# A chunked state recurrence: its small products of two tiles and two heads put on different quarters of the matrix array, and its state kept without zero blocks

## The chip, the cores and the metric

The kernel runs on one core of a Trainium2 chip. A core has a matrix engine (TensorE, PE in the profile, with PEld for its weight loads), VectorE (DVE), ScalarE (ACT), GpSimd (POOL) and SyncE (SP, which issues the transfers here). The metric is the device time of one execution in microseconds (us), the median of several runs.

## The reference

Two layers of width 2048 over 256 tokens. The first layer's mixer is the recurrence with which the change deals: per head of 64, a state S of 64 x 64 that is decayed, corrected by a rank-one term and fed with v k at each token.

```python
def step(S, inp):
    r_t, w_t, k_t, v_t, a_t, b_t = inp
    sa = jnp.einsum('bhij,bhj->bhi', S, a_t)
    S = S * w_t[:, :, None, :] + sa[..., None] * b_t[:, :, None, :] + v_t[..., None] * k_t[:, :, None, :]
    y = jnp.einsum('bhij,bhj->bhi', S, r_t)
    return S, y
```

Around it stand projections of x (r, k, v and three low-rank ones), a group norm per head, a gate, an output projection, a layer norm and a gated MLP; the second layer has differential attention in the place of the recurrence. All is float32 in and out.

## The kernel before

Activations lie with features on the 128 partitions, 16 feature tiles of 128 x 256 tokens. The large products ("dense" below) split each float32 operand into two parts, hi and lo: weights arrive in `raw` by a transfer, ScalarE casts them to `hi` (L210), VectorE or, for every fourth piece in the recurrence, GpSimd subtracts to get `lo` (L213), and TensorE multiplies (L221 to L223, or L225 and L226, into the tile `psd`).

The recurrence works on 8 groups of 2 feature tiles (index `jj`), that is 4 heads (2 per tile, index `h`, in partition rows 0 to 63 and 64 to 127), in 4 chunks of 64 tokens (index `c`). A group passes through four stages: `products` (dense, r and k), `front` (gates, decays; L1127 multiplies keys by queries in each chunk into `pss`, and L1129 masks that into `M`), `lanes` (the inverse of each chunk's 64 x 64 triangle, by small products L1217 to L1244, kept in `M`) and `chain` with `outputs`. In `pipeline` four groups are in work at once, one in each stage (the conditions for the first and last steps are left out here):

```python
todo.append((_then(self.chain(i), self.outputs(i)), PACE["chain"], PACE["chain0"]))
todo.append((self.lanes(i + 1), PACE["lanes"], PACE["lanes0"]))
todo.append((self.front(i + 2), PACE["front"], PACE["front0"]))
todo.append((self.products(i + 3), PACE["products"], PACE["products0"]))
```

`_together` interleaves these generators at their `yield`s, and the tile framework's scheduler then fixes each engine's order when the program is built; every engine runs its list in that order. In the last two steps `early` (first parts of the output projection, dense too) takes the place of the stages that have run out.

One chunk of `chain` is: rp = AR S + M v (L1295 and L1298, for each tile one and two products), a copy of rp to `R` (ScalarE), up = M R (L1303), a copy of up into `UV` (VectorE), then the new state from `KBT` and `UV` (L1310, and L1316 or L1320 on VectorE) and the outputs `yps` (L1324 from S, L1326 from UV). S is kept as [128, 2 tiles, 2 heads, 64] with a zero block where row half and head differ, so that one product of 128 rows serves both heads of a tile. rp and up of a chunk lie in 64 partitions, the same half for both tiles. In PSUM the recurrence has six banks: `pss` for front (2), lanes (1) and chain (1), `yps` (1) and `rp` (1); the dense products have two of their own.

A float32 product of this stage stands in the trace as two instructions (four calls at L1303 are "x8").

## Time and profile before

| | us |
|---|---|
| median of 3 runs | 2617.95 |
| the runs | 2612.49, 2617.95, 2630.53 |
| the profiled execution: its own time | 2630.53 |
| its span, first to last instruction | 2630.5 |
| TensorE busy in it | 2524.3 (96%) |
| VectorE busy | 2067.1 (79%) |
| ScalarE busy | 1642.4 (62%) |

The profiled execution is the slowest of the three runs. The recurrence's first product of a chain starts at 168.8 us and its last at 661.8 us; the rest of the time is dense products before and after it. A busy TensorE is not one at its peak: many of its busy nanoseconds in the recurrence belong to products that use a quarter of the array. Rows of the timeline give an instruction's start, and the distance of starts tells what it costs in a queue that never empties.

### The profile page before, as it was taken

Reading aid. Unit: us, or ns where it says so; the run is one execution under the profiler, and the core shown is the slowest. Engines: PE = TensorE matmul, PEld = TensorE weight load, DVE = VectorE, ACT = ScalarE, POOL = GpSimd, SP = SyncE. Lnnn points to the kernel's source line nnn. Section 1 sums busy time; section 2 is a strip of 40 time slices with the busy share of each in tenths; the row PEclk is TensorE's granted clock in tenths of the full one; section 3 lists DMA queues with packets and bytes.
Section 4 is the critical chain, followed back from the end, with each engine's and each line's share of the span. In section 5 each row is a group of like instructions: output and inputs, shape, how many; then the busy total and the mean of one; then the engine's idle time right before and its main releaser. Section 6 shows DMA issues by size and latency. Waiting matters only on the chain.

```text
span 2630.5 us, 54371 instructions
## 1 busy us (share of the span) xinstructions
PE 2524.3 (96%) x17374; PEld 2220.6 (84%) x17374; DVE 2067.1 (79%) x5108; ACT 1642.4 (62%) x4287; POOL 379.8 (14%) x457
## 2 busy tenths in 40 slices
PE   7999999999899999998899999999999999999997
PEld 6888888877788888887788999998888888888886
DVE  8977888885898777775677887778897777777776
ACT  5766455553566666664566676666676666666664
POOL 4343333331220000000111200002300000000112
PEclk9999999998999999999899999999999999999998
DMA  5544333343446555555666455555465555556664
GB/s 187 173 126 122 88 96 101 101 108 91 134 151 199 190 190 190 188 190 145 191 189 191 147 177 176 169 173 184 143 201 189 188 188 188 188 187 185 190 189 129
DMA packets 285160, 429.60 MB, mean 163 GB/s; under 512 B 69064, under 2 KB 91592, under 8 KB 284872
## 3 DMA queue, kind: packets, MB, share of 16 engines
q1 hardware_dynamic: 284872, 426.12, 53.4%
q8 instruction: 136, 2.23, 0.3%
q14 instruction: 152, 1.25, 0.2%
HBM read 419.45 MB, written 6.56 MB: 162 GB/s over the span
## 4 chain that ended last, share of the span: by engine, by line
PE 86%; DVE 7%; DMA 3%; issue 2%; ACT 1%; POOL 1%; SPq 0%; DVEq 0%; ACTq 0%; POOLq 0%
PE psd L225 41%; PE psd L226 21%; PE psd L221 3%; PE psd L223 3%; PE psd L222 3%; DVE lo L213 2%; PE pss L1127 1%; DMA raw<-in_ff_down 1%; PE psd L293 1%; PE psd L291 1%; PE psd L292 1%; DVE mx L767 1%; PE psd L891 1%; PE psd L892 1%; PE psd L890 1%
## 5 line engine op out<-in xcount | busy, mean ns | idle before, releaser
L210 ACT CAST hi<-raw 128x256 fp32r<-128x256 f32 (+1 forms) x3128 | 1229.3, 404 | 730.2 <-PE psd L225 470.8
L213 DVE TENSOR_TENSOR lo<-raw,hi 128x256 fp32r<-128x256 f32 (+1 forms) x2984 | 1291.9, 444 | 423.6 <-ACT hi L210 388.0
L225 PE MATMUL psd<-S,hi 128*128 128x512 f32 x3004 | 1058.6, 396 | 0.1
L226 PE MATMUL psd<-S,lo 128*128 128x256 f32 x3004 | 842.8, 281 | 3.4 <-DVE lo L213 3.2
L225 PEld LDWEIGHTS psd<-S,hi 128*128 128x128 f32 x3004 | 567.0, 189 | 132.6 <-ACT hi L210 1.1
L226 PEld LDWEIGHTS psd<-S,lo 128*128 128x128 f32 x3004 | 566.6, 189 | 5.0 <-DVE lo L213 3.7
L225 PE MATMUL psd<-hs,hi 128*128 128x512 f32 x1290 | 452.9, 395 | 22.7 <-ACT hi L210 22.7
L226 PE MATMUL psd<-hs,lo 128*128 128x256 f32 x1290 | 362.4, 281 | 0.7 <-DVE lo L213 0.6
L225 PEld LDWEIGHTS psd<-hs,hi 128*128 128x128 f32 x1290 | 242.7, 188 | 79.1 <-ACT hi L210 23.4
L226 PEld LDWEIGHTS psd<-hs,lo 128*128 128x128 f32 x1290 | 244.1, 189 | 1.6 <-DVE lo L213 1.5
L363 POOL COPY ln_acc<-X 128x256 f32<-128x256 f32 x4 | 2.1, 526 | 1257.4 <-DVE X L397 1257.4
L213 POOL TENSOR_TENSOR lo<-raw,hi 128x256 fp32r<-128x256 f32 x144 | 121.8, 852 | 330.2 <-ACT hi L210 253.4
L223 PE MATMUL psd<-S,lo 128*128 128x256 f32 x480 | 139.4, 290 | 15.6 <-DVE lo L213 10.0
L221 PE MATMUL psd<-S,hi 128*128 128x256 f32 x480 | 141.2, 294 | 1.5 <-ACT hi L210 1.5
L222 PE MATMUL psd<-S,hi 128*128 128x256 f32 x480 | 136.0, 283 | 0.0
L225 PE MATMUL psd<-S1r,hi 128*128 128x512 f32 x276 | 108.9, 425 | 1.3 <-DVE S1r L192 0.7
L223 PEld LDWEIGHTS psd<-S,lo 128*128 128x128 f32 x480 | 90.9, 189 | 22.4 <-DVE lo L213 14.7
L370 POOL TENSOR_TENSOR ln_acc<-ln_acc,X 128x256 f32<-128x256 f32 x49 | 40.2, 820 | 402.1 <-DVE X L409 388.6
L221 PEld LDWEIGHTS psd<-S,hi 128*128 128x128 f32 x480 | 91.1, 190 | 5.6 <-ACT hi L210 1.9
L222 PEld LDWEIGHTS psd<-S,hi 128*128 128x128 f32 x480 | 91.1, 190 | 1.7 <-issue 1.5
L221 PE MATMUL psd<-S1r,hi 128*128 128x256 f32 x284 | 87.7, 309 | 0.0
L891 PE MATMUL psd<-S,lo 128*128 128x258 f32 x256 | 77.2, 301 | 9.8 <-DVE lo L213 9.8
(295 smaller groups left out, 3921.5 us busy)
## 6 DMA issues: line engine op xcount, KB each, us to landing
raw<-in_ff_up SPq DMA_DIRECT2D x676, 256.0 KB, 3.4
raw<-in_ff_down SPq DMA_DIRECT2D x320, 256.0 KB, 2.9
raw<-in_rkv SPq DMA_DIRECT2D x192, 256.0 KB, 3.4
raw<-in_da_qk SPq DMA_DIRECT2D x122, 256.0 KB, 3.3
raw<-in_da_v SPq DMA_DIRECT2D x64, 256.0 KB, 3.0
raw<-in_da_o SPq DMA_DIRECT2D x64, 256.0 KB, 3.5
raw<-in_rw_o SPq DMA_DIRECT2D x50, 256.0 KB, 3.3
raw<-in_ff_down SPq DMA_DIRECT2D x32, 192.0 KB, 2.5
```

The source lines that it names most:

```text
L210: nc.scalar.copy(out=hi[:, :s * P], in_=r)
L213: eng.tensor_tensor(out=lo[:, :s * P], in0=r, in1=hi[:, :s * P].bitcast(F32), op=ALU.subtract)
L221: nc.tensor.matmul(ps[:, :T], lhsT=hi, rhs=xs[:, :T], start=first, stop=False)
L222: nc.tensor.matmul(ps[:, :T], lhsT=hi, rhs=xs[:, T:], start=False, stop=False)
L223: nc.tensor.matmul(ps[:, :T], lhsT=lo, rhs=xs[:, :T], start=False, stop=last)
L225: nc.tensor.matmul(ps, lhsT=hi, rhs=xs, start=first, stop=False)
L226: nc.tensor.matmul(ps[:, T:], lhsT=lo, rhs=xs[:, :T], start=False, stop=last)
L291: nc.tensor.matmul(o, lhsT=xh, rhs=hi, start=k == 0 and b == 0, stop=False)
L292: nc.tensor.matmul(o, lhsT=xh, rhs=lo, start=False, stop=False)
L293: nc.tensor.matmul(o, lhsT=xl, rhs=hi, start=False, stop=k == KT - 1 and b == T // P - 1)
L370: nc.gpsimd.tensor_tensor(out=self.ln_acc[:, hs], in0=self.ln_acc[:, hs], in1=t, op=ALU.add)
L891: nc.tensor.matmul(ps[:, 2:4 + T], lhsT=lo[:, w], rhs=x[:, 2:4 + T], start=False, stop=False)
```

## The change

It changes `front`, `chain` and their buffers; line numbers shift (L1298 becomes L1310, L1295 L1321, L1303 L1333, L1310 L1344, L1324 L1325, L1326 L1354, L1127 L1136).

- In the second tile the row halves are swapped (`half` picks the chunks of one row half: 0, 2 of the first tile with 1, 3 of the second, or the other way round). In a chunk the first tile's operands then lie in one half of the rows and the second tile's in the other.
- The state is [128, 2 tiles, 64], without zero blocks. AR S and S AR (L1321, L1325) become one product of 64 x 64 for each tile and head, each on the quarter of the array that its rows and its output's partitions give. Head 0 and head 1 sum rp in banks of their own (`b0`, `b1`).
- M v of the next chunk (L1310) is issued behind M R (L1333), the part of the output that comes from S (L1325) right behind L1321.
- R is copied by ScalarE (head 0) and VectorE (head 1), UV by ScalarE (first tile) and VectorE (second).
- The new state takes two instructions of 128 rows in place of four of 64.
- In `front` L1136 alternates between the heads, that is between row halves, with a bank each.
- PSUM: front and lanes share two banks (they had two and one); chain has `us`, `b0`, `b1` and `yps`.

Comments and docstrings are gone too. The core of the diff:

```diff
-        self.pss = {n: ctx.enter_context(tc.tile_pool(name=f"rg_{n}", bufs=b, space=bass.MemoryType.PSUM))
-                    for n, b in (("front", 2), ("lanes", 1), ("chain", 1))}
+        self.pss = ctx.enter_context(tc.tile_pool(name="rg_ps", bufs=2, space=bass.MemoryType.PSUM))
         self.psc = ctx.enter_context(tc.tile_pool(name="rg_pc", bufs=1, space=bass.MemoryType.PSUM))
         self.UV = fx.tile([P, GT, NC, 2, C], F32, name="UV")
-        self.R = fx.tile([P, 2 * GT, C], F32, name="R")
-        self.Ss = [fx.tile([P, GT, 2, C], F32, name=f"S{i}") for i in range(2)]
-        for x in self.Ss:
-            nc.gpsimd.memset(x, 0.0)
+        self.R = fx.tile([P, 2, C], F32, name="R")
+        self.Ss = [fx.tile([P, GT, C], F32, name=f"S{i}") for i in range(2)]
+        nc.gpsimd.memset(self.UV, 0.0)
...
-    def pst(self, stage):
-        return self.pss[stage].tile([P, 2 * T], F32, name="pss")
+    def pst(self):
+        return self.pss.tile([P, 2 * T], F32, name="pss")
+    def bank(self, name):
+        return self.psc.tile([P, 2 * T], F32, name=name)
+    def half(self, x, par):
+        ap = [list(d) for d in x.ap]
+        n = ap[1][0]
+        ap[1:2] = [[(5 - 2 * par) * n, 2], [2 * n, 2]]
+        return bass.AP(x.tensor, x.offset + par * n, ap)
...
-            sl = slice(par, GT * NC, 2)
-            nc.vector.tensor_tensor(out=KB[:, sl, par, :], in0=ck[:, sl, :], in1=ce[:, sl, :], op=ALU.mult)
-            nc.gpsimd.tensor_tensor(out=KB[:, sl, 1 - par, :], in0=ca[:, sl, :], in1=ce[:, sl, :], op=ALU.mult)
+            k_, a_, e_ = (self.half(x, par) for x in (ck, ca, ce))
+            nc.vector.tensor_tensor(out=self.half(KB[:, :, par, :], par), in0=k_, in1=e_, op=ALU.mult)
+            nc.gpsimd.tensor_tensor(out=self.half(KB[:, :, 1 - par, :], par), in0=a_, in1=e_, op=ALU.mult)
...
         for jj, j in js:
-            for h in range(2):
-                hr = slice(h * 64, h * 64 + 64)
-                ps = self.pst("front")
-                for n, u in enumerate((0, 2, 1, 3)):
-                    uu = jj * NC + u
+            banks = [self.pst(), self.pst()]
+            for n, c in enumerate((0, 2, 1, 3) if jj == 0 else (1, 3, 0, 2)):
+                uu = jj * NC + c
+                for h, ps in enumerate(banks):
+                    hr = slice(h * 64, h * 64 + 64)
                     nc.tensor.matmul(ps[:, n * P:(n + 1) * P], lhsT=KB[hr, uu, :, :], rhs=AR[hr, uu, :, :],
                                      start=True, stop=True)
+            for h, ps in enumerate(banks):
...
-        t, nc, psc, V = self.t, self.nc, self.psc, self.V
+        t, nc, V = self.t, self.nc, self.V
         s = self.st[g]
-        AR, M, KBT, pc, UV = s["AR"], s["M"], s["KBT"], s["pc"], self.UV
-        yps = s["y"] = psc.tile([P, GT, T], F32, name="yps")
-        ps = self.pst("chain")
-        for jj in range(GT):
-            for w in range(2):
-                nc.tensor.matmul(ps[:, (jj * 2 + w) * P:(jj * 2 + w + 1) * P], lhsT=V[:, g * GT + jj, w * P:(w + 1) * P],
-                                 rhs=t.x("cent"), start=True, stop=True)
+        AR, M, KBT, pc, UV, R = s["AR"], s["M"], s["KBT"], s["pc"], self.UV, self.R
+        yps = s["y"] = self.psc.tile([P, GT, T], F32, name="yps")
+        us = self.bank("us")
+        for w in range(2):
+            nc.tensor.matmul(us[:, w * P:(w + 1) * P], lhsT=V[:, g * GT, w * P:(w + 1) * P], rhs=t.x("cent"),
+                             start=True, stop=True)
+        for w in range(2):
+            for hf in range(2):
+                c = 2 * w + 1 - hf
+                nc.tensor.matmul(us[hf * 64:hf * 64 + 64, (2 + w) * P:(3 + w) * P],
+                                 lhsT=V[:, g * GT + 1, c * C:(c + 1) * C], rhs=t.x("cent"), start=True, stop=True)
         UVc = UV.rearrange("p j c h v -> p (j c) (h v)")
-        psv = ps.rearrange("p (u c) -> p u c", c=P)
-        self.copy(PACE["ec"][2], UVc[0:64, 0::2, :], psv[0:64])
-        self.copy(PACE["ec"][3], UVc[64:128, 1::2, :], psv[64:128])
-        yield
-        units = [(jj, h) for jj in range(GT) for h in range(2)]
-        u4 = lambda x: x.rearrange("p (j h) v -> p j h v", j=GT)
+        usv = us.rearrange("p (j w c) -> p j w c", j=GT, c=P)
+        for hf in range(2):
+            hr = slice(hf * 64, hf * 64 + 64)
+            self.copy(PACE["ec"][2 + hf], self.half(UVc[hr], hf), usv[hr])
+        yield
+        rows = [slice(0, 64), slice(64, P)]
+        kr = lambda jj, c: rows[(c + jj) % 2]
+        ur = lambda jj, c: rows[1 - (c + jj) % 2]
+        m = lambda jj, h, c: M[:, (c + jj) % 2, jj, h, c // 2]
+        rb = [self.bank("b0"), self.bank("b1")]
+        up = us[:, 0:2 * C].rearrange("p (h v) -> p h v", h=2)
+        sp = us[:, 2 * C:4 * C].rearrange("p (j v) -> p j v", j=GT)
+        def from_v(c):
+            for h in range(2):
+                for jj in range(GT):
+                    nc.tensor.matmul(rb[h][ur(jj, c), :C], lhsT=m(jj, h, c)[kr(jj, c), :C], rhs=UV[kr(jj, c), jj, c, h, :],
+                                     start=True, stop=c == 0)
         S = None
         for c in range(NC):
-            pu = 64 if c % 2 == 0 else 0
-            ur = slice(pu, pu + 64)
-            R = self.R
-            m = lambda jj, h: M[:, c % 2, jj, h, c // 2]
-            kr = slice(64 - pu, 128 - pu)
-            bank = psc.tile([P, 2, 2 * GT, C], F32, name="rp")
-            rp, up = bank[:, 0], bank[:, 1]
+            cs = slice(c * C, (c + 1) * C)
+            if c == 0:
+                from_v(c)
+            else:
+                for jj in range(GT):
+                    for h in range(2):
+                        nc.tensor.matmul(rb[h][ur(jj, c), :C], lhsT=AR[rows[h], jj * NC + c, 0, :],
+                                         rhs=S[rows[h], jj, :], start=False, stop=True)
+                for jj in range(GT):
+                    for h in range(2):
+                        nc.tensor.matmul(yps[rows[h], jj, cs], lhsT=S[rows[h], jj, :],
+                                         rhs=AR[rows[h], jj * NC + c, 1, :], start=jj == 0, stop=False)
+            for h in range(2):
+                self.copy("AV"[h], R[:, h, :], rb[h][:, :C])
+            yield
+            for h in range(2):
+                for jj in range(GT):
+                    r = ur(jj, c)
+                    nc.tensor.matmul(up[r, h, :], lhsT=m(jj, h, c)[r, :C], rhs=R[r, h, :], start=True, stop=True)
+            if c < NC - 1:
+                from_v(c + 1)
             for jj in range(GT):
-                if c:
-                    nc.tensor.matmul(rp[ur, 2 * jj:2 * jj + 2, :], lhsT=AR[:, jj * NC + c, 0, :], rhs=S[:, jj],
-                                     start=True, stop=False)
-                for h in range(2):
-                    nc.tensor.matmul(rp[ur, 2 * jj + h, :], lhsT=m(jj, h)[kr, :C], rhs=UV[kr, jj, c, h, :],
-                                     start=c == 0, stop=c == 0 or h == 1)
-            self.copy(PACE["ec"][0], R[ur], rp[ur])
-            yield
-            for n, (jj, h) in enumerate(units):
-                nc.tensor.matmul(up[ur, n, :], lhsT=m(jj, h)[ur, :C], rhs=R[ur, n, :], start=True, stop=True)
-            self.copy(PACE["ec"][1], UV[ur, :, c, :, :], u4(up[ur]))
+                r = ur(jj, c)
+                self.copy("AV"[jj], UV[r, jj, c, :, :], up[r])
             yield
             Sn = self.Ss[(c + g * (NC - 1)) % 2]
             if c < NC - 1:
-                sp = bank[:, 0, 0:GT]
-                for jj, h in units:
-                    nc.tensor.matmul(sp[h * 64:h * 64 + 64, jj, :], lhsT=KBT[:, jj * NC + c, h * 64:h * 64 + 64],
-                                     rhs=UV[:, jj, c, h, :], start=True, stop=True)
+                for jj in range(GT):
+                    for h in range(2):
+                        nc.tensor.matmul(sp[rows[h], jj, :], lhsT=KBT[:, jj * NC + c, h * 64:h * 64 + 64],
+                                         rhs=UV[:, jj, c, h, :], start=True, stop=True)
+                if c:
+                    for jj in range(GT):
+                        nc.vector.scalar_tensor_tensor(out=Sn[:, jj, :], in0=S[:, jj, :], scalar=pc[:, jj, c, :],
+                                                       in1=sp[:, jj, :], op0=ALU.mult, op1=ALU.add)
+                else:
+                    nc.vector.tensor_copy(out=Sn, in_=sp)
+            for jj in range(GT):
                 for h in range(2):
-                    hr = slice(h * 64, h * 64 + 64)
-                    if c:
-                        for jj in range(GT):
-                            nc.vector.scalar_tensor_tensor(out=Sn[hr, jj, h, :], in0=S[hr, jj, h, :],
-                                                           scalar=pc[hr, jj, c, :], in1=sp[hr, jj, :],
-                                                           op0=ALU.mult, op1=ALU.add)
-                    else:
-                        nc.vector.tensor_copy(out=Sn[hr, :, h, :], in_=sp[hr])
-            for jj in range(GT):
-                o = yps[:, jj, c * C:(c + 1) * C]
-                if c:
-                    nc.tensor.matmul(o, lhsT=S[:, jj], rhs=AR[:, jj * NC + c, 1, :], start=True, stop=False)
-                for h in range(2):
-                    nc.tensor.matmul(o[h * 64:h * 64 + 64], lhsT=UV[:, jj, c, h, :], rhs=m(jj, h)[:, C:],
-                                     start=c == 0, stop=True)
+                    nc.tensor.matmul(yps[rows[h], jj, cs], lhsT=UV[:, jj, c, h, :], rhs=m(jj, h, c)[:, C:],
+                                     start=c == 0 and jj == 0, stop=jj == GT - 1)
             S = Sn
             yield
...
-        ps = self.pst("chain")
+        ps = self.bank("us")
```

What became of TensorE's list at the first product of a chunk (c = 1 before, c = 2 of the same group after; `S_76` and `hi`, `lo` are a dense product, `b` the banks `b0` and `b1`, a name in brackets is an engine or queue that is waited for). Before:

```order
L221 MATMUL psd<-S_76,hi 128x256 [waits Activation_49]
L1295 MATMUL rp<-S_2560,AR 64x128 [waits DVE_49,PE_49]
L1298 MATMUL rp<-UV,M 64x64 x2
L1295 MATMUL rp<-S_2560,AR 64x128
L1298 MATMUL rp<-UV,M 64x64 x2
L222 MATMUL psd<-S_76,hi 128x256
```

After:

```order
L223 MATMUL psd<-S_76,lo 128x256
L1321 MATMUL b_5345<-S_2555,AR 64x64 [waits DVE_49]
L1321 MATMUL b_5346<-S_2555,AR 64x64
L1321 MATMUL b_5345<-S_2555,AR 64x64 [waits DVE_49]
L1321 MATMUL b_5346<-S_2555,AR 64x64
L1325 MATMUL yps<-AR,S_2555 64x64 x4
L221 MATMUL psd<-S_76,hi 128x256 [waits Activation_49]
```

The four products of M v have left this place, the two wide ones of AR S have become four, and the four S AR have come up from the end of the chunk.

The next place on TensorE is the product with R, in chunk 1 of both. Before:

```order
L222 MATMUL psd<-S_76,hi 128x256
L223 MATMUL psd<-S_76,lo 128x256
L1303 MATMUL rp<-R,M 64x64 [waits Activation_49]
L1303 MATMUL rp<-R,M 64x64 x3
L221 MATMUL psd<-S_76,hi 128x256
```

After:

```order
L223 MATMUL psd<-S_76,lo 128x256
L1333 MATMUL us<-R,M 64x64 [waits Activation_49]
L1333 MATMUL us<-R,M 64x64
L1333 MATMUL us<-R,M 64x64 [waits DVE_49]
L1333 MATMUL us<-R,M 64x64
L1310 MATMUL b_5345<-UV,M 64x64 x2
L1310 MATMUL b_5346<-UV,M 64x64 x2
L221 MATMUL psd<-S_76,hi 128x256
```

M R now waits for ScalarE ahead of its first product and for VectorE ahead of its third, and M v of the next chunk follows.

VectorE's list around the copies that this product and the next wait for (chunk 1 of a group in both). Before:

```order
L213 TENSOR_TENSOR lo<-raw,hi 128x256 [waits DMAHW5_49,PE_49,Activation_49]
L1045 COPY UV<-rp 64x2x128 [waits PE_49]
L1108 SCALAR_TENSOR_TENSOR k<-t_5267,k 128x512 [waits DVE_49]
L213 TENSOR_TENSOR lo<-raw,hi 128x256 [waits Activation_49]
L213 TENSOR_TENSOR lo<-raw,hi 128x256 [waits DMAHW6_49,PE_49,Activation_49]
L1316 SCALAR_TENSOR_TENSOR S_2561<-S_2560,pc,rp 64x64 [waits PE_49]
```

After:

```order
L1111 SCALAR_TENSOR_TENSOR kk<-k,par,kk 128x256
L1043 COPY R<-b_5346 128x64 [waits PE_49]
L1113 TENSOR_SCALAR t_5292<-wa,par 128x256
L1125 SCALAR_TENSOR_TENSOR AR<-kk,Lx 128x8x64 [waits DVE_49]
L1117 SCALAR_TENSOR_TENSOR k<-t_5292,k 128x512 [waits DVE_49]
L213 TENSOR_TENSOR lo<-raw,hi 128x256 [waits DMAHW5_49,PE_49,Activation_49]
L1043 COPY UV<-us 64x128 [waits Activation_49]
L213 TENSOR_TENSOR lo<-raw,hi 128x256
```

The copy of R for head 1 has come into this list, and the copy of UV waits for ScalarE, which copies the first tile's half out of the same bank; behind it stand the `lo` pieces of dense weights.

The in-chunk products of `front`, with `mid_83` a gate's product ahead of them. Before:

```order
L222 MATMUL psd<-mid_83,l_5717 128x256
L223 MATMUL psd<-mid_83,l_5717 128x256
L1127 MATMUL pss<-AR,KB 128x128 [waits PE_49]
L1127 MATMUL pss<-AR,KB 128x128 x3
L221 MATMUL psd<-S1r,hi 128x256 [waits Activation_49]
```

After:

```order
L222 MATMUL psd<-mid_83,l_5755 128x256
L223 MATMUL psd<-mid_83,l_5755 128x256
L1136 MATMUL pss<-AR,KB 128x128 [waits PE_49] x2
L1136 MATMUL pss<-AR,KB 128x128 x6
L221 MATMUL psd<-S1r,hi 128x256
```

A run of four calls has become a run of eight that needs two banks free, and there are two such runs in a group where there were four.

## Rows read from the trace of the kernel before

**Rows 1.** Two stretches: PE, PEld, DVE, ACT, POOL busy us, PEclk, DMA share, GB/s.

```profile
386.00:440.00 54.00, 51.90 (x600) 44.60 (x598) 45.14 (x108) 29.85 (x68) 17.99 (x22) 1.00 0.36 97
605.00:664.00 59.00, 57.61 (x517) 43.57 (x515) 34.45 (x91) 20.99 (x51) 9.41 (x12) 0.80 0.29 83
```

**Rows 2.** TensorE's timeline: start us, us, what, count, around a product with R.

```profile
379.93 0.28 PE L222 MATMUL psd<-S,hi 128*128 128x256 f32 x1
380.05 0.28 PE L223 MATMUL psd<-S,lo 128*128 128x256 f32 x1
380.25 0.68 PE L1303 MATMUL rp<-R,M 64*64 64x64 f32 x8
380.86 0.39 PE L221 MATMUL psd<-S,hi 128*128 128x256 f32 x1
381.08 0.28 PE L222 MATMUL psd<-S,hi 128*128 128x256 f32 x1
```

**Rows 3.** The same view: the state and output products, then the next chunk's rp.

```profile
382.26 0.28 PE L223 MATMUL psd<-S,lo 128*128 128x256 f32 x1
382.47 0.45 PE L1310 MATMUL rp<-UV,KBT 128*64 128x64 f32 x8
382.85 0.43 PE L1324 MATMUL yps<-AR,S 128*128 128x64 f32 x2
...
384.33 0.28 PE L222 MATMUL psd<-S,hi 128*128 128x256 f32 x1
...
385.53 0.28 PE L223 MATMUL psd<-S,lo 128*128 128x256 f32 x1
385.74 0.43 PE L1295 MATMUL rp<-S,AR 128*64 128x128 f32 x2
386.10 0.44 PE L1298 MATMUL rp<-UV,M 64*64 64x64 f32 x4
386.47 0.43 PE L1295 MATMUL rp<-S,AR 128*64 128x128 f32 x2
...
387.43 0.28 PE L222 MATMUL psd<-S,hi 128*128 128x256 f32 x1
```

**Rows 4.** The same view: state and output products of a chunk 0.

```profile
537.02 0.28 PE L226 MATMUL psd<-S1r,lo 128*128 128x256 f32 x1
537.23 0.45 PE L1310 MATMUL rp<-UV,KBT 128*64 128x64 f32 x8
537.51 0.40 PE L1326 MATMUL yps<-M,UV 128*64 128x64 f32 x8
...
538.06 0.40 PE L225 MATMUL psd<-S1r,hi 128*128 128x512 f32 x1
```

**Rows 5.** The same view: products of 32 x 32 in `lanes`.

```profile
358.27 0.73 PE L1217 MATMUL pss<-T,M 32*32 32x16 f32 x64
...
362.93 0.69 PE L1235 MATMUL pss<-T,M 32*32 32x32 f32 x32
```

**Rows 6.** The same view: one run of front's in-chunk products, and what follows.

```profile
290.41 1.16 PE L1127 MATMUL pss<-AR,KB 64*128 64x128 f32 x8
291.49 0.39 PE L221 MATMUL psd<-S1r,hi 128*128 128x256 f32 x1
```

**Rows 7.** VectorE's groups, 386 to 440 us: count, busy us, mean ns, idle before.

```profile
L213 DVE TENSOR_TENSOR lo<-raw,hi 128x256 fp32r<-128x256 f32 x24 | 12.7, 556 | 2.2 <-ACT hi L210 2.0
...
L1316 DVE SCALAR_TENSOR_TENSOR S<-S,pc,rp 64x64 f32<-64x64 f32 x8 | 1.9, 277 | 0.3 <-PE rp L1310 0.2
L1045 DVE COPY UV<-rp 64x256 f32<-64x256 f32 x4 | 1.7, 420 | 1.4 <-PE rp L1303 1.4
...
L1343 DVE SCALAR_TENSOR_TENSOR o_y<-yps,par,o_rs 128x256 f32<-128x256 f32 x2 | 1.0, 480 | 2.6 <-ACT o_rs L1045 2.6
...
L1045 DVE COPY Z<-pss 128x128 f32<-128x128 f32 x1 | 0.3, 292 | 0.0
```

**Rows 8.** TensorE's timeline: the last product of `lanes`, idle time in brackets.

```profile
366.28 0.69 PE L1244 MATMUL pss<-W,Z 32*32 32x32 f32 x32 [1.03 <-DVE Z L1238]
```

**Rows 9.** Line L1310, all of it: TensorE's idle us before it, times, by releaser.

```profile
  DVE UV L1045: 1.0, 3
```

More of the change, by code (lines that the diff above doesn't have):

```diff
@@ L1146, in front @@
         yield
-        ps = self.pst("front")
+        ps = self.pst()
         nc.tensor.matmul(ps, lhsT=t.x("bd1"), rhs=_fl(r), start=True, stop=True)
@@ L1186, in lanes @@
         for u in range(0, GT * NC, 4):
-            ps = self.pst("lanes")
+            ps = self.pst()
             for w in range(4):
@@ L1211, in lanes @@
         nc.vector.transpose(out=T1.rearrange("p u t -> p (u t)"), in_=W1.rearrange("p u t -> p (u t)"))
[L1212 removed]
+        ps = self.pst()
         pv = ps[:, :P].rearrange("p (u t) -> p u t", t=16)
@@ L1219, in lanes @@
         yield
-        ps = self.pst("lanes")
+        ps = self.pst()
         pv = ps[:, :P].rearrange("p (u t) -> p u t", t=16)
@@ L1230, in lanes @@
         Z2 = g1.tile([P, 8, 32], F32, name="Z2")
-        ps = self.pst("lanes")
+        ps = self.pst()
         pv = ps[:, :T].rearrange("p (u t) -> p u t", t=32)
@@ L1239, in lanes @@
         yield
-        ps = self.pst("lanes")
+        ps = self.pst()
         pv = ps[:, :T].rearrange("p (u t) -> p u t", t=32)
```

5 lines of the change are left out of this document (2 added, 3 removed).

## Prediction

> **What bounds the kernel now.** I looked first at where the recurrence lies and how full each engine is there. In one period of the pipeline (54 us, one group through every stage) TensorE is busy 51.9 us, VectorE 45.1, ScalarE 29.9 [rows 1]. So TensorE sets the pace and VectorE has 8.9 us to spare. The period repeats for 8 groups; in the last stretch (605 to 664 us) the granted clock averages 0.80 and VectorE is busy only 34.5 of 59 us, so TensorE alone sets it there.
>
> Then I looked at how TensorE spends a period, by the distance of starts in its timeline. A dense product of 256 columns costs 0.12 us (379.93 to 380.05 [rows 2]). I price a run of small products by what it adds between dense ones: from the start of the last dense product before it to the start of the second after it, less two times 0.12.
> - Product with R (L1303, 8 instructions): 380.05 to 381.08 is 1.03, less 0.24: 0.79 us [rows 2].
> - State and outputs (L1310, L1324, L1326): 382.26 to 384.33: 2.07, less 0.24: 1.83 us [rows 3].
> - rp (L1295, L1298): 385.53 to 387.43: 1.90, less 0.24: 1.66 us [rows 3].
>
> A chunk with a state thus takes 4.28 us of TensorE. What one instruction costs inside a run: four L1298 take 0.37 (386.10 to 386.47 [rows 3]) and eight L1303 0.61 (380.25 to 380.86 [rows 2]), so four more cost 0.24, 0.06 each. The rest of a run, 0.79 - 8 x 0.058 = 0.33, is its start and end, where the array changes over.
>
> The row on which the change stands is another: in a chunk 0 eight L1310 and eight L1326, 16 instructions, cost 537.02 to 538.06 = 1.04, less 0.24: 0.80 us [rows 4], as much as eight L1303. These alternate between two column halves of the array, and two go for the price of one. L1303 and L1298 stay on one quarter. So a slot of 0.058 us holds one product on one quarter, or two on different ones.
>
> **The change part by part.**
>
> *Chain, before.* Chunk 0 has no state: two runs of 0.79 (L1298, L1303) and one of 0.80 make 2.4. Chunks 1 and 2: 4.28 each. Chunk 3 lacks L1310 (four slots, 0.23): 4.05. A group: 15.0 us. Three of its runs touch runs of other stages and share a start (0.2 each), so 14.4.
>
> *Chain, after, if products on different quarters share a slot.* The price is 0.33 + 0.058 x slots. rp with S (L1321) and S AR (L1325): 16 instructions, 8 slots, 0.80, and no change of array shape inside, where four came before. Product with R and M v of the next chunk (L1333, L1310): 8 slots, 0.80. State and outputs (L1344, L1354): 8 slots, 0.80, as in [rows 4]. Chunk 0: M v alone 4 slots, 0.56, and two runs of 0.80: 2.16. Chunk 1: 2.4. Chunk 2: 2.4 and one more start, 0.33, since its outputs stand in two pieces: 2.73. Chunk 3: 0.80, 0.56, 0.56: 1.92. Sum 9.2. It saves 14.4 - 9.2 = 5.2 us a group.
>
> *If they do not share a slot*, L1321 with L1325 and L1333 with L1310 take 16 slots (1.26), and a group comes to 12.5: it saves 1.9. No row shows quarters of 64 x 64 side by side. The nearest are the 32 x 32 products on the diagonal: 64 in 0.73 us (four positions), 32 in 0.69 (two) [rows 5], so 0.011 and 0.022 us each. Those differ in rows and columns like the pairs of L1333, L1310 and L1325. I take sharing.
>
> The Trainium skill (TensorEngine Tiling (Array Packing), Restrictions and Gotchas) speaks against that: different row tiles cannot access the same PSUM bank simultaneously, and L1333, L1325 and each half of L1310 pair row tiles in one bank. The four row positions of L1217 write one bank too, and 64 in 0.73 us could not go one by one at L1303's price [rows 2, 5], so here the trace disagrees; by the rule the saving is the 1.9.
>
> *In-chunk products.* Eight L1127 run 1.08 us from start to start of what follows [rows 6], 1.28 with start and end; there are four such runs in a group, two of which touch others. After there are two of 16 instructions. If row halves share slots, each costs what eight do now: two runs go, 2.3 us. If not, only two starts go: 0.5. No row shows two row halves over the same columns; I take 2.3, by the nearest [rows 4], where it is the column halves that share.
>
> *Lanes and centering.* Runs are cut into more pieces (v centered by 2 full and 4 half-wide products, L1244's successor in two): two more starts, 0.6 us. Against it the wait of 1.03 us at L1244 for VectorE's Z [rows 8] has more dense products in front of it. With two shared banks, front's first product waits for VectorE to empty what lanes wrote, which can put that wait back. From -1 to +1.5 us a group; I take none, as a wait that moves.
>
> *VectorE.* Before, a group has four UV copies of 0.42, eight state updates of 0.277 [rows 7] and two state copies, at most 0.29 each by the copy of 128 x 128 [rows 7]: 4.5 us. After: four R copies and four UV copies of at most 0.29, four updates of 0.277, one copy of 0.29: 3.7. It saves 0.8: 44.3 busy. ScalarE gains about four copies of under 0.4, beside 24 us to spare [rows 1]. The change adds one wait here: VectorE's UV copy waits for ScalarE's, out of the same bank. Behind it stand `lo` pieces that dense products need. ScalarE's copy is the same size, so about 0.3 us, four times: 1.2 us idle. One fill of UV in place of two of S, on GpSimd, comes once and is covered.
>
> *Sum.* TensorE would need 54.0 - 5.2 - 2.3 = 46.5 us a period. VectorE needs 44.3 busy, the 2.6 us in which it waits for ScalarE's gate copy [rows 7], which no step of the change shortens, and the new 1.2: 48.1. So VectorE is next. Of its other idle time, 8.9 - 2.6 = 6.3 us spent waiting for TensorE and for `hi`, I keep a quarter, 1.6, because TensorE is now ahead of it most of the time: 49.7. A period loses 4.3 us. Seven of them: 30. In the last group TensorE alone decides: 5.2 at full clock, by the mean clock of 0.80 some 6.5 to 7: 7. Together **37 us**.
>
> The profiled execution took 2630.5, 12.5 above the median of the runs; nothing lies around its span. I put the difference on the median: 2618 - 37 = **2581 us**.
>
> **The rivals.**
> - *VectorE never gets in the way.* For it: 44.3 busy in 46.5 fits by count. Against: both would be over 93% full with orders fixed beforehand. TensorE's 7.5 us a group, seven times, and 7: 60, so 2558.
> - *Quarters don't share slots*, the change doing what it says in the code and not on the array (the rule above gives this too). 1.9 + 0.5 = 2.4 a group, 19 in all: 2599. Against it: [rows 5].
> - *VectorE keeps its idle share.* Its waits hang on orders that the scheduler fixes: 8.9 of 54 idle. Then 44.3 busy means 53.0, 1.0 us a period; 7 and the last group's 7: 14, so 2604. For it: 2.0 us of idle time in `lo` are waits for ScalarE, not for TensorE [rows 7].
> - *Slower: VectorE late at R.* The product with R waited for ScalarE alone, which has spare time; it now waits for VectorE too, in whose list the copy stands behind pieces of 0.56 us on average [rows 7]. Between rp and it lie 12 dense products, 1.4 us of cover. Four such stops a group eat the 7.5 us if each lasts 1.9 us, that is if VectorE runs 3.3 us behind; at 2.9 us each a group loses 4.1, 33 in all: 2651. Against it: of the UV copies, which TensorE already awaits from VectorE, three stopped L1310, 1.0 us in sum [rows 9].
>
> **How the numbers follow.** The forecast 0.47, the faster rival 0.18, no sharing 0.12, VectorE's idle share 0.15, slower 0.08. Runs of this kernel spread by 0.7%, so 1% (26 us) is about what a measurement tells from no change: faster means under 2592. The forecast is taken as 2565 to 2597, three quarters of it and more under 2592 (0.38); with the faster rival (0.18) and the lucky end of the two small gains (0.04) that is 0.60. Slower by over 1% is the last rival's, 0.07 after its mild end; within 1%, 0.33. The range runs from 2552, just below the faster rival, to 2611, which takes in both small gains; left out are the slower rival and the far end of the faster one.
>
> **What the changed profile would show.** Right: L1321 and L1325 as one run of about 0.8 us, L1333 with L1310 the same; 16 instructions of L1136 in some 1.1 us; a period of 49 to 50 us with VectorE busy 89% or more of it and more TensorE idle time before `lo` products than now. Wrong on sharing: those runs at 1.2 us. Wrong on VectorE: TensorE still 96% busy at a period near 47. Wrong in sign: long idle rows ahead of L1333 or front's first products, put down to VectorE. What I can't see beforehand is the granted clock: the last group runs partly at half speed, and if the new mix of products changes when that falls, some ten us come or go.

## The result and the profile after

The changed kernel takes 2589.78 us, the median of five runs (2589.24 to 2604.3), against 2617.95 (2612.49 to 2630.53): a ratio of 0.990 with a 95% interval of 0.9878 to 0.9921, 28 us faster. 37 were forecast. The profiled execution took 2589.51 us (span 2587.7).

I mark the periods by the first product of L1375 (L1347 before), which stands once in each group. In the first fence are the engines' busy times in windows cut at these marks, after; in the second three such windows of before. The columns are those of [rows 1].

```profile
288.30:339.70 51.40, 46.32 (x630) 39.92 (x629) 44.32 (x108) 30.31 (x72) 19.39 (x24) 0.97 0.38 103
339.70:393.60 53.90, 49.55 (x631) 42.22 (x630) 45.10 (x107) 30.36 (x72) 21.50 (x22) 0.91 0.36 98
393.60:444.90 51.30, 47.97 (x630) 40.85 (x629) 43.53 (x108) 30.25 (x72) 20.33 (x22) 0.93 0.40 104
444.90:496.90 52.00, 48.04 (x631) 41.26 (x630) 44.29 (x107) 32.05 (x76) 21.36 (x23) 0.93 0.38 101
...
582.10:617.10 35.00, 34.69 (x485) 25.97 (x483) 27.38 (x72) 17.09 (x46) 7.68 (x9) 1.00 0.42 120
```

```profile
297.20:355.90 58.70, 56.15 (x603) 48.07 (x602) 46.24 (x109) 30.17 (x68) 17.64 (x23) 0.91 0.37 95
355.90:410.30 54.40, 52.31 (x603) 44.84 (x602) 45.55 (x108) 30.13 (x68) 18.00 (x23) 1.00 0.36 97
...
612.50:663.10 50.60, 49.21 (x460) 37.42 (x459) 29.38 (x76) 17.48 (x43) 7.51 (x9) 0.76 0.28 83
```

Three things are to be seen. TensorE's work in a period fell from 52.3 us to some 46 (46.3 in the window with the highest clock). The period fell only to 51.3 to 53.9. And the granted clock is under 1.00 in all four steady windows, where before had 1.00 in most of that place (0.91 from 297.2 to 355.9): by these averages 3 to 10 us of each were spent at the half level. In the last group it is the other way round: before ran 24 of 50.6 us at half the clock, after none. So this pair of profiles shows too little gain in the steady periods and too much at the end; the experiments below give the period at full clock, 51.1 against 54.4 (50.0 to 52.2 in the edits that neither add work nor leave any out).

The clock also tells which engine the period waits for. Before, some 10 us at the half level made a period 4.3 us longer (58.7 against 54.4). In the changed kernel some 27 us of it in four periods cost about 3.5: they last 208.6 us together, and four periods of heads_apart below, all at full clock, 205.1. So TensorE's speed decides much less of the period than it did before.

The runs of small products, as in [rows 2 to 4], TensorE's timeline:

```profile
417.91 0.28 PE L223 MATMUL psd<-S,lo 128*128 128x256 f32 x1
418.12 0.27 PE L1333 MATMUL us<-R,M 64*64 64x64 f32 x2
418.14 0.27 PE L1310 MATMUL b<-UV,M 64*64 64x64 f32 x2
418.23 0.23 PE L1333 MATMUL us<-R,M 64*64 64x64 f32 x2
418.25 0.22 PE L1310 MATMUL b<-UV,M 64*64 64x64 f32 x2
...
418.52 0.39 PE L221 MATMUL psd<-S,hi 128*128 128x256 f32 x1
418.75 0.28 PE L222 MATMUL psd<-S,hi 128*128 128x256 f32 x1
...
419.92 0.28 PE L223 MATMUL psd<-S,lo 128*128 128x256 f32 x1
420.13 0.45 PE L1344 MATMUL us<-UV,KBT 128*64 128x64 f32 x8
420.41 0.40 PE L1354 MATMUL yps<-M,UV 128*64 128x64 f32 x8
420.74 0.38 PE L221 MATMUL psd<-S,hi 128*128 128x256 f32 x1
420.96 0.28 PE L222 MATMUL psd<-S,hi 128*128 128x256 f32 x1
...
422.14 0.28 PE L223 MATMUL psd<-S,lo 128*128 128x256 f32 x1
424.34 0.47 PE L1321 MATMUL b<-S,AR 64*64 64x64 f32 x6 [1.92 <-DVE S L1348]
```

Priced as the prediction does, by starts less 0.24: L1333 with L1310 adds 418.75 - 417.91 - 0.24 = 0.60 us (0.80 forecast), L1344 with L1354 0.80 (0.80). Five runs of L1321 with L1325 that wait for nothing add 0.70 in the median, and 16 instructions of L1136 1.29 (forecast 1.28). The sharing is there, and four quarters are even better than two.

The last row shows the other side: TensorE stands 1.92 us for the state S. VectorE's timeline says why:

```profile
419.57 2.39 DVE L1123 TENSOR_TENSOR KB<-k,wa 128x256 f32<-128x256 f32 x2
421.88 0.95 DVE L213 TENSOR_TENSOR lo<-raw,hi 128x256 fp32r<-128x256 f32 x1
422.76 1.21 DVE L1127 TENSOR_TENSOR AR<-r,eL 128x512 f32<-128x512 f32 x1
424.00 0.47 DVE L1348 SCALAR_TENSOR_TENSOR S<-S,pc,us 128x64 f32<-128x64 f32 x2
```

L1344 was done by 420.6, and the update of S could have begun then; in VectorE's fixed list it stands behind front's pieces and a `lo`. Behind TensorE's pause, at 425.5, the granted clock falls to its half level (1.2 GHz): the dense products start 0.20 us apart there and not 0.12. TensorE's waits in four steady periods of after (288.3 to 497; us in total, times, the longest):

```profile
PE b L1321 <- DVE S L1348: 6.9, 4, 1.9
PE pss L1254 <- DVE Z L1248: 3.9, 4, 1.3
PE yps L1354 <- ACT UV L1043: 1.8, 2, 1.6
PE pss L1091 <- DVE M L1261: 1.1, 2, 0.9
PE us L1344 <- DVE UV L1043: 1.0, 1, 1.0
```

### The profile page after: what moved, and what is told of

It reads as the page before. It is cut to its first block, busy times and chain, and to the rows that moved or that the text cites. A ratio compares the mean times of both kernels' runs of the same rounds, so it can differ in the third digit from the quotient of the medians.

```text
span 2587.7 us, 54801 instructions
## 1 busy us (share of the span) xinstructions
PE 2469.0 (95%) x17598; PEld 2173.1 (84%) x17598; DVE 2056.9 (79%) x5100; ACT 1643.8 (64%) x4319; POOL 391.0 (15%) x456
## 4 chain that ended last, share of the span: by engine, by line
PE 79%; DVE 5%; DMA 2%; issue 1%; ACT 1%; POOL 0%; DVEq 0%; ACTq 0%; SPq 0%; POOLq 0%
PE psd L225 41%; PE psd L226 21%; PE psd L221 2%; PE psd L223 2%; PE psd L222 2%; DMA dtab<-tab 1%; PE psd L293 1%; PE psd L291 1%; PE psd L292 1%; DVE lo L213 1%; PE psd L891 1%; PE psd L890 1%; PE psd L892 1%; PE lnst L345 1%; PE pss L1136 0%
## 5 line engine op out<-in xcount | busy, mean ns | idle before, releaser
L213 POOL TENSOR_TENSOR lo<-raw,hi 128x256 fp32r<-128x256 f32 x144 | 132.9, 929 | 297.3 <-ACT hi L210 226.7
L223 PE MATMUL psd<-S,lo 128*128 128x256 f32 x480 | 140.2, 292 | 14.3 <-DVE lo L213 8.9
L222 PE MATMUL psd<-S,hi 128*128 128x256 f32 x480 | 142.0, 296 | 0.0
L221 PE MATMUL psd<-S,hi 128*128 128x256 f32 x480 | 140.8, 293 | 0.5 <-ACT hi L210 0.5
L223 PEld LDWEIGHTS psd<-S,lo 128*128 128x128 f32 x480 | 92.5, 193 | 23.3 <-DVE lo L213 13.4
```

What stands on the lines that cost most here:

```text
L213: eng.tensor_tensor(out=lo[:, :s * P], in0=r, in1=hi[:, :s * P].bitcast(F32), op=ALU.subtract)
L221: nc.tensor.matmul(ps[:, :T], lhsT=hi, rhs=xs[:, :T], start=first, stop=False)
L222: nc.tensor.matmul(ps[:, :T], lhsT=hi, rhs=xs[:, T:], start=False, stop=False)
L223: nc.tensor.matmul(ps[:, :T], lhsT=lo, rhs=xs[:, :T], start=False, stop=last)
```

## The experiments

The texts on record weigh these against each other. Theory 1: what TensorE saved is real, but in a steady period VectorE and ScalarE decide much of the end. Theory 2: two full stretches of VectorE's list lie on the chain. Theory 3: VectorE's work and its waits set the period. The rivals: A, TensorE still sets it; B, quarters share nothing; C, two engines that read one bank cost the gain; D, VectorE's sum at a constant idle share; E, single waits between engines.

All twelve are edits of the changed kernel. The time of each is given as its ratio to the kernel before on the same chip; the changed kernel's own is 0.9900. Beside it stands the length of the steady periods in the trace. A period at full clock is one with a granted clock of 1.00 over its whole window.

**1. quarters_apart**: the same products, one quarter after another.

```
-            for h in range(2):
-                for jj in range(GT):
+            for jj in range(GT):
+                for h in range(2):
                     nc.tensor.matmul(up[r, h, :], ...
(the other way round at L1325, L1344, L1354; L1310 as here)
```

> The changed kernel with its small products in another order: the products of one quarter of the array follow one another, where they alternated between quarters (only L1321, whose four products stand on four quarters, keeps its order). The instructions and their number are the same. Priced by 0.33 + 0.058 us x slots, a chunk's runs grow by 0.23 (L1325), 0.66 (L1333 with L1310) and 0.45 (L1344 with L1354), some 4.7 us a group. Theory 1 (sharing is what was saved, but in a steady period VectorE and ScalarE decide much of the end): 1.5 to 3 us in each of the five steady periods and the whole 4.7 in the last two, 15 to 25 us slower than the changed kernel's 2590. Rival A (TensorE still sets every period): 4.7 x 8 = 38 us slower, 2627. Rival B (quarters share nothing; what was saved is starts of runs): the same time, 2590, and the same price of the runs.

0.9897 (0.9879 to 0.9916), no difference. L1333 with L1310 adds 0.61 us, L1321 with L1325 0.74, L1344 with L1354 0.86. My expectation fell, but not towards rival B: the order in the program is not the order on the array. L1333's four products stand ahead of L1310's in TensorE's list, and in the trace the two lines start by turns, as in the rows above. The edit therefore didn't take the sharing away; experiment 3 does.

**2. heads_apart**: the in-chunk products, head by head.

```
-            for n, c in enumerate(...):
-                for h, ps in enumerate(banks):
+            for h, ps in enumerate(banks):
+                for n, c in enumerate(...):
```

> The changed kernel with the in-chunk products (L1136) of one head after those of the other, so that its two row halves don't alternate. If row halves share slots, two runs of 16 instructions grow from 1.29 to about 2.2 us each, 1.9 us of TensorE a group; if they don't, nothing grows. Theory 1 (VectorE decides where front's work lies): less than half of it arrives, 3 to 8 us slower than 2590. Rival A (TensorE sets the period): 15 us slower.

0.9918 (0.9902 to 0.9934). Sixteen L1136 add 1.83 us in place of 1.29, so row halves over the same columns do share, and in blocks of eight they share less. The five us of time are within the intervals, which overlap, and the four steady periods, all at full clock, last 51.1 to 51.4 us, as long as those of experiment 3: 1.1 us more of TensorE a period did not lengthen them.

**3. same_quarters**: M v on the quarters of the product with R. The text on record says which data it reads instead.

```
-  lhsT=m(jj, h, c)[kr(jj, c), :C], rhs=UV[kr(jj, c), jj, c, h, :]
+  lhsT=m(jj, h, c)[kr(jj, c + 1), :C], rhs=UV[kr(jj, c + 1), jj, c, h, :]
```

> The changed kernel with M v (L1310) reading the other row half, so that it stands on the same two quarters as the product with R (L1333) beside it and not on the other two. What it multiplies there is other data: the recurrence's values are not the reference's, the work is as much. If quarters work side by side as counted, 16 instructions on two quarters take eight slots, and the run of L1333 with L1310 adds 0.8 us in place of 0.60 (on one quarter each: 1.26). Rival B (quarters share nothing): 0.60 as before. The period doesn't change by theory 2 (0.2 x 3 us of TensorE a group go into waits that are there), +5 us if TensorE sets it.

TensorE's timeline in this kernel:

```profile
463.68 0.28 PE L223 MATMUL psd<-S,lo 128*128 128x256 f32 x1
463.89 0.45 PE L1333 MATMUL us<-R,M 64*64 64x64 f32 x8
464.17 0.40 PE L1310 MATMUL b<-UV,M 64*64 64x64 f32 x8
464.50 0.39 PE L221 MATMUL psd<-S,hi 128*128 128x256 f32 x1
464.73 0.28 PE L222 MATMUL psd<-S,hi 128*128 128x256 f32 x1
```

464.73 - 463.68 - 0.24 = 0.81 us, as counted for eight slots, against 0.60 on four quarters; rival B is out. The ratio is 0.9878 (0.9859 to 0.9897), not slower, and its periods at full clock are 51.1, 50.6, 51.1 and 51.4 us. This is the nearest to a clean measure of the changed kernel's steady period, of which no window ran wholly at full clock: 51.1 us with TensorE 46.2 and VectorE 44.7 busy (and 0.6 us more of TensorE's work a group than the changed kernel has).

**4. kb_vector**: all of KB on VectorE.

```
-  nc.gpsimd.tensor_tensor(out=self.half(KB[:, :, 1 - par, :], par), ...
+  nc.vector.tensor_tensor(out=self.half(KB[:, :, 1 - par, :], par), ...
```

> The changed kernel with all four pieces of KB on VectorE, where two of them were GpSimd's. On VectorE the two pieces take 1.23 us each beside GpSimd's, and AR behind them 1.21 where the other AR takes 0.68. Theory 1 says that VectorE's list sets this stretch of a period, and takes the length of these pieces to come from GpSimd working beside them: four pieces of about 0.45 and AR at 0.68 are 2.5 us in place of 3.6, some 1 us a period, 4 to 8 us faster than 2590. If a piece is 1.2 us long by itself, VectorE gets 2.4 us more a group and the kernel is 10 to 19 us slower. If VectorE's list decides nothing (rival A), no difference.

Groups of VectorE in 325 to 482 us, after and then this kernel:

```profile
L1123 DVE TENSOR_TENSOR KB<-k,wa 128x256 f32<-128x256 f32 x6 | 7.2, 1233 | 0.0
L1127 DVE TENSOR_TENSOR AR<-r,eL 128x512 f32<-128x512 f32 x3 | 3.6, 1206 | 0.0
```

```profile
L1123 DVE TENSOR_TENSOR KB<-k,wa 128x256 f32<-128x256 f32 x6 | 2.5, 414 | 0.0
L1127 DVE TENSOR_TENSOR AR<-r,eL 128x512 f32<-128x512 f32 x3 | 2.0, 678 | 0.0
```

The pieces shrink to a third and to half, as thought; with the six pieces that VectorE has taken over (L1124, 3.6 us) its KB and AR take 8.1 us where they took 10.8. The ratio stays at 0.9899 (0.9881 to 0.9917). TensorE's wait at L1321 for S fell from 6.9 us to 1.9 (270 to 620 us), and the one at L1354 for ScalarE's UV rose from 3.3 to 10.2. In this pair of profiles one wait gave way to the next.

**5. copies_scalar**: `"AV"` becomes `"AA"` in the copies of R and UV.

> The changed kernel with all copies of R and UV in the chain on ScalarE, where VectorE had one of each pair: 2.0 us a group less on VectorE, and no pair of engines that waits at one bank. Two copies in a row on ScalarE make each of eight steps some 0.3 us longer. Theory 1: VectorE's list is shorter, but ScalarE's UV copy is already what TensorE waits for at L1354 (8.6 us in 12 waits), so -5 to +5 us. Rival C (two engines reading one bank for R and UV are what costs the gain): 8 us faster or more.

0.9907 (0.989 to 0.9924), nothing won. VectorE loses eight copies a group, 2.0 us, and is busy 43.4 us in the mean of the four steady periods, against 44.3. Its `lo` pieces take 0.521 us on average (325 to 482 us) where the changed kernel's take 0.484, but that can't be put down to the edit: same_quarters has as much work on VectorE as the changed kernel, and 0.551 (there GpSimd's own `lo` pieces take 0.85 us, in the changed kernel 1.18). Rival C fell.

**6 and 7. fill_packed and fill_slack**: four more products on VectorE a group, in two places.

```
+  for _ in range(4):
+      nc.vector.tensor_tensor(out=self.fill, in0=f, in1=f, op=ALU.mult)
(f: 512 columns of KB after L1127, or of UV after the last chunk's UV copy)
```

> The changed kernel with four extra products on VectorE a group (128x512, some 0.68 us each, 2.7 us together), behind front's KB and AR. They write a tile that nobody reads. Theory 2 (a period is set by a chain that goes through two full stretches of VectorE's list, outputs and lanes about 9 us, front's KB and AR about 9 us, and through TensorE in between): this stretch is on the chain, so most of the 2.7 us arrives in each of some six periods: +10 to +17 us against the changed kernel. Rival A (TensorE sets the period, VectorE has 8 us to spare): 0 to 3 us.

> The same four extra products, 2.7 us of VectorE a group, but behind the UV copy of the last chunk, where VectorE waits for ScalarE's first parts (hi) and for o_rs. Theory 2 (it depends on the place, not on VectorE's sum): 0 to 5 us against the changed kernel. Rival D (VectorE's busy time as a sum sets the period, at a constant idle share of 15%): as much as with the other place, 2.7 x 8 = 22 us, and more by the idle share.

0.9945 (0.9923 to 0.9966) and 0.9948 (0.9931 to 0.9964): 12 us each, of 22 us of added work. The place made no difference, so theory 2 fell; the sum rule of rival D would have cost twice as much. The periods with the filler in the slack run from 53.1 to 55.1 us (53.2 at full clock), those of the packed place from 49.8 (full clock) to 55.6 (clock 0.91). They scatter too much to say where in a period the 12 us went.

**8. wc_scalar**: `wc='PVVA'` becomes `'AAAA'`.

> The changed kernel with the four copies of M's quarters (L1259, 32x256) on ScalarE, where two were VectorE's (0.78 us each) and two GpSimd's. It takes 1.6 us a group out of VectorE's full stretch of outputs and lanes. Theory 2: this stretch is on the chain; 0.5 to 1.5 us a period, 4 to 10 us faster than the changed kernel, unless ScalarE's four copies (some 0.4 us each) come later than VectorE's. Rival A (TensorE sets the period): no difference.

0.9922 (0.9908 to 0.9936), 6 us slower by the medians, with intervals that overlap: against theory 2 again. One period at full clock lasts 52.2 us.

**9. less_tensor**: 3.8 us of TensorE a group left out.

```
-  nc.tensor.matmul(ps[:, :T], lhsT=hi, rhs=xs[:, T:], start=False, stop=False)
+  if not short:
+      nc.tensor.matmul(ps[:, :T], lhsT=hi, rhs=xs[:, T:], start=False, stop=False)
```

> The changed kernel without one of the three dense products (L222, the first part of the weights by the second part of the data) of the k projection: 32 products of 0.119 us, 3.8 us of TensorE a group, are left out, and k loses its lower digits. ScalarE and VectorE make the same parts as before. Theory 3 (a steady period is VectorE's 44.6 us of work and some 6.5 us in which it waits for ScalarE's hi, for o_rs and for TensorE; TensorE's need of 46 is not the bound): 50 to 51 us a period, 0 to 8 us faster than the changed kernel. Rival A (TensorE sets it): a period of 47.3, 8 x 3.8 = 30 us faster.

0.9904 (0.9886 to 0.9921): thirty us less of TensorE's work, and no time won. Its steady periods:

```profile
290.50:339.70 49.20, 46.74 (x598) 38.19 (x598) 43.89 (x107) 30.48 (x72) 17.88 (x22) 0.93 0.40 106
339.70:392.90 53.20, 49.97 (x598) 40.72 (x597) 43.46 (x107) 30.16 (x72) 18.79 (x22) 0.87 0.38 99
392.90:448.30 55.40, 52.48 (x599) 42.16 (x598) 43.50 (x107) 30.20 (x72) 19.02 (x23) 0.82 0.36 96
448.30:498.20 49.90, 44.42 (x599) 35.98 (x598) 46.05 (x108) 31.65 (x76) 18.91 (x22) 1.00 0.41 107
```

At full clock one period of 49.9 us, 1.2 less than 51.1, for 3.8 us of work, and 50.0 occurs without this edit too (copies_scalar). The first, with 7 us at the half level, lasts 49.2; the second and third ran 14 and 20 us at that level and are 53.2 and 55.4 us long. TensorE got a new wait: it stands before `lo` of the dense products (L224 here, L223 else) ten times, 6.4 us in all from 270 to 620 us, and in the changed kernel not once there. Over its four runs the mean clock is 0.968 to 0.978; the runs of the kernel before on that chip had 0.979 to 0.986. Against the changed kernel's 0.979 in the median that hides some 10 us at the most, not the 30 of rival A.

**10. w0_355**: five buffers for hi and lo (`w0=(3, 4, 4)` becomes `(3, 5, 5)`).

> The changed kernel with five buffers in place of four for hi and for lo, all through the kernel. In a steady period ScalarE stands 8 us before hi for TensorE (a buffer that is still read), and VectorE 2.7 us before lo for hi. Theory 3: these waits are part of what is added to VectorE's work, 0.5 to 2 us a period less, 4 to 14 us faster in the recurrence. If ScalarE's wait only shows that it is ahead: no difference there. Outside of the recurrence the same edit can do something too; that is read from the trace by stage.

0.9955 (0.9938 to 0.9973), slower by 14 us. The profiled execution of it was 9 us under its median, with steady periods of 50.0 to 53.0 us, so it doesn't show where the loss lies; that stays open. A gain in the recurrence is not seen.

**11. pool3**: every third lo on GpSimd (`pool=4` becomes 3).

> The changed kernel with every third lo on GpSimd in the recurrence, where it was every fourth: 2.7 of 24 pieces a period less on VectorE (0.48 us each, 1.3 us), 2.7 of 0.85 us more on GpSimd. No more for ScalarE, unlike the earlier edits that took work off VectorE. Theory 3: up to 1.3 us a period, 0 to 9 us faster; but VectorE's pieces are longer while GpSimd works, some 10 us a period over their shortest, and if that grows with GpSimd's time, it takes back 2.3 us x 0.5 = 1.2: no difference. Rival A (TensorE sets the period): no difference.

0.9906 (0.9894 to 0.9919), no difference. Some 2.7 pieces a period left VectorE, 1.3 us, and it is busy 44.3 us a period, as before. The pieces that remain take 0.566 us on average in place of 0.484, which is near the 0.551 of same_quarters, where none were taken away.

**12. less_vector**: 4.7 us of VectorE a group left out.

```
-        for i in range(1, 16):
+        for i in (1, 2, 3, 6, 9, 12, 15):
```

> The changed kernel with 8 of the 15 steps of the triangular inverse in lanes (L1203 and L1205) left out: 16 instructions and 4.7 us of VectorE a group, by their durations; the inverse is then not whole. Nothing changes on ScalarE, TensorE or GpSimd. It is the counterpart of the run with 3.8 us less on TensorE. Theory 3 (VectorE's work and its waits set a period at full clock, 51.1 us): 3 to 4.7 us a period less, down to the 47 where TensorE's need of 46 takes over; 20 to 32 us faster than the changed kernel. Rival E (neither engine's sum: single waits between the engines, that stay where they are): 0 to 1 us a period, under 8 us. Rival A (TensorE sets the period): no difference.

0.9874 (0.9854 to 0.9895), 7 us below the changed kernel, and the intervals overlap. The first and third of its steady periods:

```profile
294.40:346.10 51.70, 46.92 (x630) 40.20 (x629) 41.12 (x91) 30.51 (x72) 18.34 (x22) 0.97 0.38 102
400.30:452.30 52.00, 47.10 (x631) 40.34 (x630) 41.73 (x91) 30.57 (x72) 18.54 (x22) 0.97 0.38 102
```

The second lasts 54.2 us at a clock of 0.91, the fourth 51.9 at 0.97; none ran wholly at full clock. VectorE is busy 41.1 to 42.1 us, has some 10 to spare, and the period is no shorter: at the same clock of 0.97 the changed kernel has 51.4, quarters_apart 51.0 to 51.3. Theory 3 fell too; of the texts on record rival E is what is left, by elimination: neither engine's sum decides, but single waits between engines. Why 2.7 us of filler on VectorE cost 12 us and 4.7 us left out win 7 at the most is not shown.

What these waits are is best seen in heads_apart, whose periods are alike and at full clock (303.3 to 508.4 us, four periods):

```profile
PE yps L1354 <- ACT UV L1043: 6.5, 4, 1.6
PE b L1321 <- DVE S L1348: 5.5, 4, 1.4
PE pss L1091 <- DVE M L1261: 3.2, 4, 1.2
PE pss L1254 <- DVE Z L1248: 3.0, 4, 0.9
```

Four waits, once a period each, 18.2 / 4 = 4.6 us. TensorE's 46.3 busy and these make 50.8 of 51.3. ScalarE's timeline shows how the first of them comes about, ahead of the L1354 at 388.70:

```profile
386.86 0.51 ACT L1155 ACTIVATE r<-r,par 128x256 f32<-128x256 f32 x1 [2.08 <-POOL r L1153]
387.27 0.39 ACT L210 CAST hi<-raw 128x256 fp32r<-128x256 f32 x1
387.57 0.50 ACT L1155 ACTIVATE r<-r,par 128x256 f32<-128x256 f32 x1
387.98 0.39 ACT L210 CAST hi<-raw 128x256 fp32r<-128x256 f32 x1
388.39 0.26 ACT L1043 COPY UV<-us 64x128 f32<-64x128 f32 x1
```

ScalarE waits 2.08 us for GpSimd's r, a piece of front that TensorE takes only 29 us later (L1158 at 417.11), and the UV copy that TensorE needs at once stands four places behind it. GpSimd's r in turn waits for VectorE's AR. Moving the UV copy ahead of L1155 and S ahead of KB in those lists wasn't tried. So that these waits set the period is argued and not shown; kb_vector shows only that a shorter list ahead of S shortens the wait for S. No edit that keeps the arithmetic is faster than the changed kernel by more than the intervals allow.

## Why the prediction was right, and where it was off

The sign and the range were right; the gain was put at 37 us and is 28. Of the two readings behind it, TensorE's saving was right, and that VectorE's work comes next was not.

- *Prices of the runs*: right, or too careful. Runs of 0.60, 0.70 and 0.80 stand where 0.80 was taken for each; by them the chain is some 8.5 us a group, not 9.2. L1136 hit its 1.28. Rival "quarters don't share slots" is refuted by experiment 3: 0.60 us on four quarters, 0.81 on two, where one each would take 1.26. The rule of the Trainium skill (TensorEngine Tiling (Array Packing), Restrictions and Gotchas) that different row tiles cannot access one PSUM bank at the same time is not refuted by this, and no run here tests it. At the pace of the dense products (0.12 us for 256 columns) 64 columns take 0.03 us, an estimate; L1333's eight into the bank `us`, 0.24 of the run's 0.27 without start and end, may have come one by one while L1310 filled the banks `b`. At that pace the 64 products of 16 columns in [rows 5] take 0.48 of their 0.73 us one by one, so the prediction's disagreement with the rule does not follow from them either. What failed is the price of 1.9 us that was hung on the rule.
- *TensorE's need, 46.5 us*: the number is right (busy 46.2 us a period in same_quarters, 45.5 to 46.5 in other periods at full clock), in part by luck. The 7.5 us were taken off the period of 54.0, which holds 2.1 us of waits, and not off the 52 of work. The saving itself holds: priced as above and without the waits in them, the runs with products of the chain or L1136 add 20.1 us in the period before (410.3 to 464.6) and 12.4 to 12.6 at full clock after (quarters_apart, same_quarters), 7.4 to 7.7 less. But the other small products, lanes and centering, went from 6.0 to 7.1 us, which the prediction put at nothing, and TensorE's busy time fell by 6.1 and not 7.5.
- *VectorE busy 44.3 us*: right (43.5 to 45.1 in the four steady windows).
- *"So VectorE is next", 48.1 plus a quarter of its other idle time, a period of 49.7*: this step failed, by 1.4 us a period, about 10 us in seven. The period is 51.1 at full clock, and not because VectorE has that much to do: with 4.7 us less it stays (less_vector), and with 3.8 us less on TensorE it loses 1.2 at the most (less_tensor). Two of the signs that the prediction named for being right are missing: VectorE is busy 84 to 86% of the four periods and not 89 or more, and TensorE's idle time before `lo` of dense products, 2.6 us from 297 to 519 before, did not grow but is gone (288 to 497). TensorE had 2.2 us of named waits a period before (8.8 in 297 to 519) and has about 4.6 now: results that came in time while TensorE was slower now come late. For S and UV the rows above show them behind front's pieces in the fixed lists of VectorE and ScalarE; M and Z were not followed. The rival with VectorE's idle share, 53.0, was 1.9 us off on the other side.
- *The new wait of VectorE for ScalarE's UV copy, 1.2 us a group*: 0.3 us in three periods (325 to 482 us). TensorE waits at L1354 for ScalarE's copy itself.
- *The slower rival, VectorE late at R*: right in kind, wrong in place. L1333 hardly waits (ScalarE's R once, 0.3 us); S, and UV on ScalarE, are late.
- *Lanes, taken as none*: the wait for Z went from 1.0 us (3.1 in three) to 1.0 (3.9 in four), and one for M at L1091 of up to 1.2 came with it.
- *The last group, 7 us*: the pair of profiles shows 15.6 (50.6 to 35.0), but 24 us at half clock in before's go into that; they account for up to 12. At full clock it is nearer to 4, an estimate from the two windows.
- *The granted clock*, which I said I couldn't see: the changed kernel's five runs have a mean clock of 0.974 to 0.981, 0.979 in the median, and those of the kernel before, beside the first experiments, 0.982 in the median. Three thousandths are 8 us of 2590 at the most. So part of the missing gain may lie there (not in this pair of profiles, which have 0.979 before and 0.980 after), and the runs don't separate it from the period's 10 us: the two overlap.

At full clock the parts add up to some 32 us, near the measured 28: 3.3 in each of four steady periods (13), 4 to 5 in the fifth (51.1 to 46.3 in same_quarters), 4.4 in the sixth (42.4 to 38.0), some 4 in the last, and about 6 up to the first mark (297.2 to 288.3, of which I take 3 off for 7 us more at half clock before). Behind the last mark the changed kernel takes 3.3 us more than before (1970.6 against 1967.3), which leaves some 29; why is not shown.

## What to carry to other kernels

When an engine that sets the pace gets faster, don't size the next bound by the busiest engine's sum alone: list the short results that the fast engine takes from others in each round, and look what stands ahead of each in the producer's fixed list. Here four of them, 0.8 to 1.6 us each, account for nearly half of what TensorE saved (6.1 us of work a period, 3.3 of time), and in kb_vector and less_tensor, where one engine got less to do, another result became the late one. Compare periods at the same granted clock before believing a difference of 2 us in 50.

## What the runs showed of the hardware that was not expected

- Products on different quarters of the array do not start in program order: four L1333 ahead of four L1310 in the list start by turns in the trace, and the run costs 0.60 or 0.61 us in either order. L1136 with eight instructions in a row on one row half costs 1.83 us, alternating 1.29.
- VectorE's pieces are longer while GpSimd works: L1123 takes 1.23 us in the mean beside GpSimd's work and 0.41 without it, L1127 1.21 and 0.68. In the four steady periods of the changed kernel the durations of VectorE's instructions exceed the shortest of the same line and shape by 7.3 to 8.8 us, 6.6 to 8.1 of it in instructions that overlap one on GpSimd. Which engine bears it differs from kernel to kernel: in the changed kernel a `lo` piece takes 0.48 us on VectorE and 1.18 on GpSimd, in same_quarters 0.55 and 0.85. The Trainium skill (SBUF — State Buffer, SBUF: two separate sides) describes a pair of ports that VectorE and GpSimd lock against each other for a whole instruction; the trace agrees: the two L1123 at 419.57 and 421.01 us of the changed kernel take 1.51 and 0.95 us, and each ends 0.28 us after the end of the GpSimd instruction beside which it began (L1116, of 1.48 us, and L1124, of 0.80).
- With 3.8 us a group of TensorE's work left out, the mean granted clock was 0.968 to 0.978 and that of whole windows 0.82 and 0.87; those windows are 2 to 4 us longer than a period of 51.1 at full clock with the work in it.
- The spread between runs goes with the clock: the kernel before took 2617.86 us at a mean clock of 0.987 and 2630.15 at 0.979 on one chip.
